# Transposing the gated FFN tiles of a hybrid trunk layer by DMA in 16-bit halves

## The chip, the cores and the metric

The kernel runs on one core of a Trainium2 chip. The metric is the device time of one execution in microseconds (us), median of the runs. All arithmetic of the layer is float32; nothing is computed on the host.

## The reference

One layer on `x` of 256 tokens by 2048 features, with `D_FF` = 5504: a half-step SwiGLU FFN, a mixer, a second half-step FFN, each between two RMS norms. The change touches the two FFNs alone.

```python
def rms_norm(x, w):
    y = xf * lax.rsqrt(jnp.mean(xf * xf, axis=-1, keepdims=True) + EPS)
    return (y * w.astype(jnp.float32)).astype(x.dtype)

def swiglu(x, w_gate, w_up, w_down):
    return (jax.nn.silu(x @ w_gate) * (x @ w_up)) @ w_down

def reference(...):
    f1 = swiglu(rms_norm(h, ffn1_pre_norm[l]), ffn1_w_gate[l], ffn1_w_up[l], ffn1_w_down[l])
    h = h + 0.5 * rms_norm(f1, ffn1_post_norm[l])
    m = hybrid_token_mixer(rms_norm(h, mix_pre_norm[l]), ...)
    h = h + rms_norm(m, mix_post_norm[l])
    f2 = swiglu(rms_norm(h, ffn2_pre_norm[l]), ffn2_w_gate[l], ffn2_w_up[l], ffn2_w_down[l])
    h = h + 0.5 * rms_norm(f2, ffn2_post_norm[l])
    return h
```

## The kernel before

The 256 tokens are two tiles `t` of 128 partitions. Every float32 matmul is three matmuls in the type float32r: a weight chunk `raw` is rounded on ScalarE to `whi` (line 151), VectorE takes the rest `wlo = raw - whi` (line 153), and `mm3` adds `xhi*whi`, `xlo*whi` and `xhi*wlo` (lines 157 to 159). The activations are kept transposed (`xhi`, `xlo`: features on partitions), since a matmul contracts over partitions.

An FFN goes over `D_FF` in ten blocks of 512 columns and one of 384 (`for f0`). In a block, `gemm_pair` makes the gate `g` and the up product `u` of both token tiles from 16 row blocks of each weight. Most row blocks are taken in plain steps (12 matmuls of a chunk of 1024 columns). Some are taken in steps of `seven`, in which seven products stand for eight: VectorE first makes sums of weights in `wsum` (line 243), ScalarE rounds `raw` and `wsum` (`whi` at lines 278 and 282, `wsumh` at 280 and 284), and VectorE takes the rests (`wlo` twice, `wsuml` once, all at line 243); TensorE then has 21 matmuls. Blocks alternate between three such steps (`SUMS`) and four (`FOUR`). At a block's end VectorE adds shared sums into the four results (`c<-c,psum`). The ring of `raw`, `whi` and `wlo` has five buffers each; `wsum`, `wsumh` and `wsuml` share a ring of three, so a step's `wsumh` waits until TensorE has read the last step's.

A block's end is then: ScalarE makes `silu` of the gate (line 728), and a generator `finish` per token tile does the rest. Its first step runs at once: VectorE multiplies `u`, the norm's factor and the silu into `hn` (line 703). Two of the generator's steps later TensorE transposes `hn` in pieces of 128x128 (line 397, four per tile, three in the last block) into a PSUM tile, and ScalarE copies that into `hT` (line 709), whose tiles stay in SBUF until the down projection splits them into `hkhi` and `hklo`. `side.pump()` after every plain step, and twice in a seven-product step, advances all generators by one step; `side.flush()` in the down projection's second step runs the last two to their end.

In each engine's queue the instructions stand in an order that a scheduler makes at build time from the order of the code and its own estimates, so a changed instruction also moves its neighbours; each engine then works off its queue in order. Weight loads are issued from SP's queue, a few others from ScalarE's. DMAs take eight completion semaphores in turn.

Of the kernel before, what the change touches and what calls it, by code (L numbers as in the profile page):

```python
# [7 lines left out]
F32 = mybir.dt.float32  # L8
F32R = mybir.dt.float32r
BF16 = mybir.dt.bfloat16  # L10
U8 = mybir.dt.uint8
AF = mybir.ActivationFunctionType
ALU = mybir.AluOpType
AX = mybir.AxisListType

P = 128
# [6 lines left out]
CB = 512  # L23
# [63 lines left out]
def kernel(ctx: ExitStack, tc: tile.TileContext, a: dict, out: bass.AP):  # L87
    nc = tc.nc
# [8 lines left out]
    work = ctx.enter_context(tc.tile_pool(name="work", bufs=2))  # L97
# [5 lines left out]
    def nm(s):  # L103
        uid[0] += 1
        return f"{s}_{uid[0]}"

    def ps_tile(s="ps"):
        return psum.tile([P, CB], F32, tag="ps", name=nm(s))

    h = [[hpool.tile([P, CB], F32, name=f"h{t}_{n}") for n in range(4)] for t in range(NT)]  # L110
# [13 lines left out]
    def ring_alloc(w):  # L124
        hi, lo = [ring.tile([P, RW], F32R, tag=s, name=nm(s))[:, :2 * w]
                  .rearrange("p (i c) -> p i c", i=2) for s in ("whi", "wlo")]
        return [(hi, lo)]
# [22 lines left out]
    def split_into(hi, lo, src):  # L150
        last[0] = nc.scalar.activation(hi, src, AF.Copy)  # L151
        with tc.issue_after(first_ops.pop().ins) if first_ops else nullcontext():
            nc.vector.tensor_tensor(lo, src, hi.bitcast(F32), op=ALU.subtract)  # L153
# [7 lines left out]
    def gemm_block(w_dram, c0, w, lhs, nkt=KT, held=None, raws=(), ready=()):  # L161

        raws, ready = list(raws), list(ready)
        nb = -(-w // CB)
        step = 2 // nb
        pss = [[ps_tile(f"mm{t}") for _ in range(nb)] for t in range(NT)]

        def chunk(k0, alloc):
            if ready:
                return ready.pop(0)
            raw = raws.pop(0) if raws else None
            src = w_dram[k0 * P:(k0 + step) * P, c0:c0 + w]
            return wchunk(src.rearrange("(k p) c -> p k c", p=P) if nb == 1 else
                          src.rearrange("p (n c) -> p n c", n=nb), w // nb, alloc, raw)

        def mm(t, k0, parts):
            for i, part in enumerate(parts):  # L180
                kt = k0 + i % step
                mm3(pss[t][i // step][:, :w // nb], lhs(t, kt), part, kt == 0, kt == nkt - 1)

        if held is None:
            for k0 in range(0, nkt, step):
                parts = chunk(k0, ring_alloc)
                for t in range(NT):
                    mm(t, k0, parts)
                side.pump()
        else:  # L190
            kept = []
            for i, k0 in enumerate(range(0, nkt, 2)):
                kept.append((k0, chunk(k0, ring_alloc if i < RING else held)))
                mm(0, *kept[-1])
                side.pump()
            for k in kept:
                mm(1, *k)
                side.pump()
            side.flush()
        return pss if nb > 1 else [ps[0] for ps in pss]  # L200
# [41 lines left out]
    def add(o, x, y, op=ALU.add):  # L242
        return nc.vector.tensor_tensor(o, x, y, op=op)  # L243

    class Blocks:
# [19 lines left out]
        def seven(self, u, end):  # L265
# [11 lines left out]
            (ahi, alo), (bhi, blo) = ring_alloc(w) + ring_alloc(w)  # L277
            nc.scalar.activation(ahi, ra, AF.Copy)  # L278
            add(wsum[:, 0:2, :], ra, rb[:, 0:1, :].broadcast_to([P, 2, w]))
            nc.scalar.activation(hi[:, 0:2, :], wsum[:, 0:2, :], AF.Copy)  # L280
            add(rb[:, 0, :], wsum[:, 0, :], ra[:, 1, :])
            nc.scalar.activation(bhi, rb, AF.Copy)  # L282
            summed = add(wsum[:, 2, :], rb[:, 0, :], rb[:, 1, :])
            last[0] = nc.scalar.activation(hi[:, 2, :], wsum[:, 2, :], AF.Copy)  # L284
            with tc.issue_after(summed.ins):
# [43 lines left out]
    def gemm_pair(ws, w, lhs, sums, ready=(), following=(), raws=(), sevens=SUMS,  # L329
                  late=False):  # L330

        raws = list(raws)
        nu = KT // 2

        b = Blocks(lambda i, kt: ws[i][0][kt * P:(kt + 1) * P, ws[i][1]:ws[i][1] + w],
                   w, lhs, part_of(sums))

        def split(i, k0):
            return wchunk(None, w, raw=raws.pop(0)) if raws else first_of(*ws[i], w)(k0 // 2)

        steps = [(u, i) for u in range(nu) if u not in sevens for i in range(2)]
        if late:
            at = range(6, 6 + 2 * len(sevens), 2)
        elif len(sevens) > len(SUMS):
            at = range(3, 3 + 2 * len(sevens), 2)  # L350
        else:
            at = [2 * u - j for j, u in enumerate(sevens)]
        for j, u in zip(at, sevens):
            steps.insert(j, (u, None))
        ready = list(ready)
        for j, (u, i) in enumerate(steps):
            side.fast = late
            if any(i is None for _, i in steps[j:j + 2]):
                side.full = True
            if i is None:  # L360
                b.seven(u, u == sevens[-1])
                continue
            k0 = 2 * u
            parts = ready.pop(0) if ready else split(i, k0)
            if (u, i) == (nu - 1, 0) and sevens:
                ready = [split(1, k0)]
                b.share()
            for t in range(NT):
                b.plain((k0, k0 + 1), t, i, parts, u == nu - 1)
            side.pump()  # L370
        ready = [chunk(0) for chunk in following]
        for i in range(2 if sevens else 0):
            for t in range(NT):
                b.close(t, i)
        side.full = side.fast = False
        return *[[b.c[t][i] for t in range(NT)] for i in range(2)], ready
# [18 lines left out]
    def transpose4(dst_ps, src, n=4):  # L395
        for i in range(n):
            end = nc.tensor.transpose(dst_ps[:, i * P:(i + 1) * P], src[:, i * P:(i + 1) * P],  # L397
                                      ident)
        return end

    def tiles4(x):
        return x.rearrange("p (k c) -> p k c", c=P)

    def new_xT():
        x = [None] * NT, [None] * NT, [0] * NT
        for t in range(NT):
            alloc_xT(x, t)
        return x
# [41 lines left out]
    def square(src, ss, n):  # L450
        sq = work.tile([P, CB], BF16, tag="sq", name=nm("sq"), bufs=1)
        nc.scalar.activation(sq, src, AF.Square, accum_out=ss[:, n:n + 1])

# [221 lines left out]
    def ffn(pre, x, rs, post, pre_next, begin=None, ready=(), then=None):  # L675
        with ExitStack() as fctx:
            fwork = fctx.enter_context(tc.tile_pool(name=nm("fwork"), bufs=2, reuse_waits="tile"))
# [19 lines left out]
            hT = []  # L697
# [1 line left out]
            fours = 0 if begin else 1  # L699

            def finish(t, f0, w, u, s):
                hn = fwork.tile([P, CB], F32, tag="hn", name=nm("hn"))
                nc.vector.scalar_tensor_tensor(hn[:, :w], u[:, :w], rs[t], s[:, :w],
                                               op0=ALU.mult, op1=ALU.mult)
                yield
                yield
                tp = ps_tile()
                transpose4(tp, hn, w // P)
                nc.scalar.activation(hT[f0 // CB][:, :w // P, t * P:(t + 1) * P],
                                     tiles4(tp[:, :w]), AF.Copy)  # L710

            for f0 in range(0, DFF, CB):
                w = min(CB, DFF - f0)
# [3 lines left out]
                if f0 or begin:  # L717
                    g, u, ready = gemm_pair(
                        [(a[pre + "_w_gate"], f0), (a[pre + "_w_up"], f0)], w, xl, sums, ready,
                        following, () if f0 else raws,  # L720
                        (FOUR if f0 // CB % 2 == fours else SUMS) if f0 else ())
# [3 lines left out]
                s = []  # L725
# [4 lines left out]
                if not (f0 or begin):  # L730
                    side.spawn(x_sums())
                    u = gemm_block(a[pre + "_w_up"], f0, w, xl)
# [40 lines left out]
                v = in_x("xhi1", F32R)  # L773
                return [(v[:, 0:2, :], v[:, 2:4, :])]

            ytags = ["hn", "hn", "silu", "silu"]

            def ys():
                return fwork.tile([P, CB], F32, tag=ytags.pop(), name=nm("y"))
# [6 lines left out]
    def mixer(x, rs, ready, following):  # L786
        xl = lhs_of(x)
        w_in = a["w_in"]
        with ExitStack() as mctx:
# [339 lines left out]
            for r0 in range(0, P, 32):  # L1129
                nc.vector.tensor_copy(diag[r0:r0 + 32, :], ident[r0:r0 + 32, r0:r0 + 32])  # L1130
            masks = mp.tile([P, masked, 4, 16], U8, name="masks")
            for i in range(4):
# [138 lines left out]
    x, rs = new_xT(), [None, None]  # L1271

    def begin(x_sums):
# [27 lines left out]
        def idling(n):  # L1301
            for _ in range(n):
# [7 lines left out]
        return raws  # L1310

    x, rs, ready = ffn("ffn1", x, rs, "ffn1_post_norm", wcols[:, 1, :], begin,
                       then=first_of(a["w_in"], O_GQ))
    x, rs, ready = mixer(x, rs, ready, first_of(a["ffn2_w_gate"], 0))
    ffn("ffn2", x, rs, "ffn2_post_norm", None, ready=ready)
    side.flush()

# [45 lines left out]
```

## Time and profile before

| | |
|---|---|
| runs | 2080.27 us median of 3 (2080.07 to 2080.61) |
| the profiled execution | 2080.67 us, its span 2078.8 us |
| granted TensorE clock over the span | 0.999 |
| first FFN, blocks | about 10 to 444 us |
| first FFN, down projection | about 444 to 685 us |
| mixer | about 685 to 1390 us |
| second FFN, blocks, then down projection | about 1390 to 1850 us, then to the end |

Times in a view are us from the span's start. In a row of the order of time stand the start, the duration, the engine, the line, the operation and `out<-in` by the program's names; `x2` is two equal instructions merged; in brackets stands the idle time just before it and what ended it. PE is TensorE's matmuls, PEld its weight loads, DVE VectorE, ACT ScalarE; an engine name with q is its queue, where DMAs are issued. Matmuls overlap: a 512-column matmul is shown with 0.39 us, while the next starts 0.23 us later.

### The profile page before, as it was taken

What the parts mean: (1) busy time and instruction counts of PE and PEld (TensorE: products, weight loads), DVE (VectorE), ACT (ScalarE), POOL (GpSimd) and SP (SyncE); (2) the same over time, 40 slices, a digit from 0 to 9 for tenths busy, and PEclk for the clock granted to TensorE, in tenths of its full rate; (3) what the DMA queues carried; (4) which work ended last, traced back from release to release, by engine and by line L of the source; (5) the groups of instructions that cost most, each with busy time, mean ns of one, the idle gap of its engine ahead of it and who ended that gap; (6) DMA issues with size and microseconds to landing.
All of it is one profiled execution on the core that took longest, in us unless ns stands there. A gap on an engine that the chain in (4) does not pass through costs nothing.

```text
span 2078.8 us, 29319 instructions
## 1 busy us (share of the span) xinstructions
PE 2067.8 (99%) x10509; PEld 1721.1 (83%) x10509; DVE 1854.7 (89%) x2187; ACT 1239.7 (60%) x1670; POOL 40.6 (2%) x87
## 2 busy tenths in 40 slices
PE   9999999999999999999999999999999999999998
PEld 7888888898888888878888888888888888898886
DVE  7898999989999879989999897578999989999896
ACT  6555656565666576576655554465555655666663
POOL 1000000000000100000000000010000000000000
PEclk9999999999999999999999999999999999999999
DMA  8566656656667467555565666755666657576663
GB/s 267 183 210 199 211 188 194 214 183 226 208 195 233 153 192 232 163 168 188 174 203 186 184 221 214 220 179 172 222 200 186 209 186 224 165 239 201 198 208 132
DMA packets 200665, 412.23 MB, mean 198 GB/s; under 512 B 18036, under 2 KB 26423, under 8 KB 200520
## 3 DMA queue, kind: packets, MB, share of 16 engines
q1 hardware_dynamic: 194896, 401.80, 61.0%
q10 hardware_dynamic: 5624, 8.57, 1.3%
q8 instruction: 82, 1.34, 0.3%
q14 instruction: 63, 0.52, 0.1%
HBM read 406.11 MB, written 4.19 MB: 197 GB/s over the span
## 4 chain that ended last, share of the span: by engine, by line
PE 96%; ACT 1%; DVE 1%; issue 0%; DMA 0%; POOL 0%; SPq 0%; DVEq 0%; POOLq 0%; ACTq 0%
PE c L157 22%; PE c L159 21%; PE c L158 21%; PE p L159 5%; PE p L158 5%; PE p L157 5%; PE mm L157 3%; PE mm L159 3%; PE mm L158 3%; PE ps L397 2%; PE acc L157 1%; PE acc L158 1%; PE acc L159 1%; PE ps L905 0%; DVE h L510 0%
## 5 line engine op out<-in xcount | busy, mean ns | idle before, releaser
L151 ACT ACTIVATE whi<-raw 128x1024 fp32r<-128x1024 f32 (+3 forms) x498 | 510.6, 1033 | 279.8 <-PE c L158 114.7
L153 DVE TENSOR_TENSOR wlo<-raw,whi 128x1024 fp32r<-128x1024 f32 (+3 forms) x498 | 587.5, 1190 | 86.6 <-ACT whi L151 85.3
L157 PE MATMUL c<-whi,xhi 128*128 128x512 f32 (+1 forms) x1270 | 495.8, 391 | 0.5 <-DVE hq L849 0.3
L159 PE MATMUL c<-wlo,xhi 128*128 128x512 f32 (+1 forms) x1270 | 490.8, 387 | 0.0
L158 PE MATMUL c<-whi,xlo 128*128 128x512 f32 (+1 forms) x1270 | 490.5, 386 | 0.0
L243 DVE TENSOR_TENSOR wlo<-raw,whi 128x1024 fp32r<-128x1024 f32 (+1 forms) x252 | 294.5, 1203 | 11.9 <-ACT whi L278 6.3
L159 PEld LDWEIGHTS c<-wlo,xhi 128*128 128x128 f32 x1270 | 238.4, 188 | 47.2 <-DVE wlo L153 0.3
L157 PEld LDWEIGHTS c<-whi,xhi 128*128 128x128 f32 x1270 | 238.5, 188 | 46.9 <-issue 0.7
L158 PEld LDWEIGHTS c<-whi,xlo 128*128 128x128 f32 x1270 | 238.6, 188 | 44.9
L282 ACT ACTIVATE whi<-raw 128x1024 fp32r<-128x1024 f32 (+1 forms) x126 | 131.8, 1046 | 204.5 <-DVE raw L243 78.5
L243 DVE TENSOR_TENSOR wsuml<-wsum,wsumh 128x1536 fp32r<-128x1536 f32 (+1 forms) x126 | 218.0, 1730 | 33.7 <-ACT wsumh L284 33.6
L157 PE MATMUL c<-whi,hkhi 128*128 128x512 f32 x558 | 217.0, 389 | 0.0
L159 PE MATMUL c<-wlo,hkhi 128*128 128x512 f32 x558 | 216.8, 388 | 0.0
L158 PE MATMUL c<-whi,hklo 128*128 128x512 f32 x558 | 216.7, 388 | 0.0
L280 ACT ACTIVATE wsumh<-wsum 128x1024 fp32r<-128x1024 f32 (+1 forms) x126 | 131.5, 1044 | 108.6 <-DVE wsum L243 74.7
L278 ACT ACTIVATE whi<-raw 128x1024 fp32r<-128x1024 f32 (+1 forms) x126 | 131.4, 1043 | 100.2 <-PE c L158 84.7
L243 DVE TENSOR_TENSOR wsum<-raw,raw 128x1024 f32<-128x1024 f32 (+1 forms) x126 | 151.8, 1205 | 20.5 <-DMA raw<-in_ffn_w_down_dram 17.3
L159 PEld LDWEIGHTS c<-wlo,hkhi 128*128 128x128 f32 x558 | 104.8, 188 | 21.6
L158 PEld LDWEIGHTS c<-whi,hklo 128*128 128x128 f32 x558 | 104.8, 188 | 21.3
L157 PEld LDWEIGHTS c<-whi,hkhi 128*128 128x128 f32 x558 | 104.8, 188 | 21.3
L243 DVE TENSOR_TENSOR c<-c,psum 128x512 f32<-128x512 f32 (+1 forms) x135 | 86.6, 682 | 11.8 <-PE c L159 11.4
L243 DVE TENSOR_TENSOR wsum<-raw 128x512 f32<-128x512 f32 (+1 forms) x126 | 86.0, 683 | 3.6
(347 smaller groups left out, 3117.1 us busy)
## 6 DMA issues: line engine op xcount, KB each, us to landing
raw<-in_ffn_w_down_dram SPq DMA_DIRECT2D x124, 512.0 KB, 4.6
raw<-in_w_in_dram SPq DMA_DIRECT2D x104, 512.0 KB, 4.5
raw<-in_ffn_w_up_dram SPq DMA_DIRECT2D x97, 512.0 KB, 4.5
raw<-in_ffn_w_gate_dram SPq DMA_DIRECT2D x96, 512.0 KB, 4.7
raw<-in_ffn_w_gate_dram SPq DMA_DIRECT2D x128, 256.0 KB, 3.8
raw<-in_w_in_dram SPq DMA_DIRECT2D x128, 256.0 KB, 3.5
raw<-in_ffn_w_up_dram SPq DMA_DIRECT2D x126, 256.0 KB, 3.8
raw<-in_ffn_w_down_dram SPq DMA_DIRECT2D x96, 256.0 KB, 4.0
```

The source lines that it names most:

```text
L151: last[0] = nc.scalar.activation(hi, src, AF.Copy)
L153: nc.vector.tensor_tensor(lo, src, hi.bitcast(F32), op=ALU.subtract)
L157: nc.tensor.matmul(ps, lhsT=xhi, rhs=whi, start=start, stop=False)
L158: nc.tensor.matmul(ps, lhsT=xlo, rhs=whi, start=False, stop=False)
L159: nc.tensor.matmul(ps, lhsT=xhi, rhs=wlo, start=False, stop=stop)
L243: return nc.vector.tensor_tensor(o, x, y, op=op)
L278: nc.scalar.activation(ahi, ra, AF.Copy)
L280: nc.scalar.activation(hi[:, 0:2, :], wsum[:, 0:2, :], AF.Copy)
L282: nc.scalar.activation(bhi, rb, AF.Copy)
L397: end = nc.tensor.transpose(dst_ps[:, i * P:(i + 1) * P], src[:, i * P:(i + 1) * P], ident)
```

## The change

`finish` no longer uses TensorE. VectorE writes the gated tile over the silu tile. ScalarE reads that tile as 16-bit words, two for each float32, and writes the low halves of all columns and then the high halves into `halves` (two planes of 512 values, as whole numbers in uint16). A DMA transpose, issued from ScalarE's queue, turns the eight blocks of 128x128 (six in the last block) into `turned`. Six generator steps later ScalarE writes the planes back into every second 16-bit word of `hT`. `turned` uses the three buffers of the tag `tmp`, and the down projection's `y` tiles use the tag `halves` where they used `hn`.

```diff
             def finish(t, f0, w, u, s):
-                hn = fwork.tile([P, CB], F32, tag="hn", name=nm("hn"))
-                nc.vector.scalar_tensor_tensor(hn[:, :w], u[:, :w], rs[t], s[:, :w],
+                n = w // P
+                nc.vector.scalar_tensor_tensor(s[:, :w], u[:, :w], rs[t], s[:, :w],
                                                op0=ALU.mult, op1=ALU.mult)
                 yield
-                yield
-                tp = ps_tile()
-                transpose4(tp, hn, w // P)
-                nc.scalar.activation(hT[f0 // CB][:, :w // P, t * P:(t + 1) * P],
-                                     tiles4(tp[:, :w]), AF.Copy)
+                halves = fwork.tile([P, 2 * CB], U16, tag="halves", name=nm("halves"))
+                nc.scalar.activation(halves[:, :2 * w].rearrange("p (h f) -> p h f", h=2),
+                                     s.bitcast(U16)[:, :2 * w].rearrange("p (f h) -> p h f", h=2),
+                                     AF.Copy)
+                turned = work.tile([P, 8, P], U16, tag="tmp", name=nm("turned"), bufs=3)
+                nc.scalar.dma_start_transpose(turned[:, :2 * n, :], halves[:, :2 * w])
+                for _ in range(6):
+                    yield
+                dst = hT[f0 // CB].bitcast(U16)[:, :n, 2 * t * P:2 * (t + 1) * P]
+                src = turned[:, :2 * n, :].rearrange("p (h j) k -> p h j k", h=2)
+                nc.scalar.activation(dst.rearrange("p j (k h) -> p h j k", h=2), src, AF.Copy)
...
-            ytags = ["hn", "hn", "silu", "silu"]
+            ytags = ["halves", "halves", "silu", "silu"]
```

The scheduler puts the new instructions so. ScalarE's queue at the start of the first FFN's third block, which has four seven-product steps (98 to 137 us), before:

```order
L280 ACTIVATE wsumh_1021<-wsum_1020 128x1024
L282 ACTIVATE whi_1029<-raw_1019 128x1024
L284 ACTIVATE wsumh_1021<-wsum_1020 128x512
L151 ACTIVATE whi_1068<-raw_1066 128x1024
L278 ACTIVATE whi_1093<-raw_1084 128x1024
L709 ACTIVATE hT_955<-ps_988 128x4x128
L709 ACTIVATE hT_955<-ps_994 128x4x128
L282 ACTIVATE whi_1095<-raw_1085 128x1024
L151 ACTIVATE whi_1130<-raw_1128 128x1024
L278 ACTIVATE whi_1155<-raw_1146 128x1024
L280 ACTIVATE wsumh_1087<-wsum_1086 128x1024
```

And with the change, at the same place. Lines from 12 on are one higher in the changed file, those behind `finish` seven; the text names lines of the kernel before.

```order
L281 ACTIVATE wsumh_1011<-wsum_1010 128x1024
L708 ACTIVATE halves_970<-silu_947 128x1024
L708 ACTIVATE halves_974<-silu_949 128x1024
L712 DMA_TRANSPOSE turned_972<-halves_970 128x8x128
L712 DMA_TRANSPOSE turned_976<-halves_974 128x8x128
L283 ACTIVATE whi_1019<-raw_1009 128x1024
L285 ACTIVATE wsumh_1011<-wsum_1010 128x512
L152 ACTIVATE whi_1058<-raw_1056 128x1024
L279 ACTIVATE whi_1083<-raw_1074 128x1024
L717 ACTIVATE hT_951<-turned_972 128x2x4x128
L717 ACTIVATE hT_951<-turned_976 128x2x4x128
L283 ACTIVATE whi_1085<-raw_1075 128x1024
```

Both `halves` and both transposes stand ahead of the step's second weight rounding; `hT` keeps its place, four activations behind the transposes. In blocks with three such steps the same four stand ahead of the first `wsumh` instead. Behind these rows ScalarE's order differs too: from the block's second seven-product step on, both `wsumh` stand ahead of the plain step's `whi`. VectorE follows; its queue in that second step, before:

```order
L243 TENSOR_TENSOR wlo_1094<-raw_1084,whi_1093 128x1024
L243 TENSOR_TENSOR wlo_1096<-raw_1085,whi_1095 128x1024
L153 TENSOR_TENSOR wlo_1131<-raw_1128,whi_1130 128x1024
L243 TENSOR_TENSOR wsuml_1088<-wsum_1086,wsumh_1087 128x1536
L243 TENSOR_TENSOR wsum_1148<-raw_1146,raw_1147 128x1024
```

With the change:

```order
L244 TENSOR_TENSOR wlo_1084<-raw_1074,whi_1083 128x1024
L244 TENSOR_TENSOR wlo_1086<-raw_1075,whi_1085 128x1024
L244 TENSOR_TENSOR wsuml_1078<-wsum_1076,wsumh_1077 128x1536
L154 TENSOR_TENSOR wlo_1123<-raw_1120,whi_1122 128x1024
L244 TENSOR_TENSOR wsum_1140<-raw_1138,raw_1139 128x1024
```

`wsuml` and the plain step's `wlo` have changed places; this is so in all steps of the four-step blocks but the first. In the first FFN's last block (384 columns) the results of the block before it are turned closer together on ScalarE, with the change:

```order
L708 ACTIVATE halves_3778<-silu_3755 128x1024
L152 ACTIVATE whi_3866<-raw_3864 128x768
L712 DMA_TRANSPOSE turned_3780<-halves_3778 128x8x128
L708 ACTIVATE halves_3782<-silu_3757 128x1024
L279 ACTIVATE whi_3891<-raw_3882 128x768
L712 DMA_TRANSPOSE turned_3784<-halves_3782 128x8x128
L717 ACTIVATE hT_3759<-turned_3780 128x2x4x128
L283 ACTIVATE whi_3893<-raw_3883 128x768
L717 ACTIVATE hT_3759<-turned_3784 128x2x4x128
```

Here and in the two down projections only one or two activations stand between a transpose and the `hT` that waits for it. TensorE's queue differs by the missing transposes alone, SP's and GpSimd's not at all.

More of the change, by code (lines that the diff above doesn't have):

```diff
@@ L11 @@
 U8 = mybir.dt.uint8
+U16 = mybir.dt.uint16
 AF = mybir.ActivationFunctionType
```

## Prediction

> **What bounds the kernel now.** I read the page's engine lines and its chain first, then two stretches of the first FFN side by side, then the order of time of each engine in them.
>
> ```profile
> PE 2067.8 (99%) x10509; PEld 1721.1 (83%) x10509; DVE 1854.7 (89%) x2187; ACT 1239.7 (60%) x1670; POOL 40.6 (2%) x87
> ...
> PE 96%; ACT 1%; DVE 1%; issue 0%; DMA 0%; POOL 0%; SPq 0%; DVEq 0%; POOLq 0%; ACTq 0%
> ```
>
> ```profile
> 98.00:137.00 39.00, 39.00 (x178) 32.37 (x177) 37.32 (x37) 22.35 (x26) 0.00 (x0) 1.00 0.60 191
> 137.00:177.00 40.00, 40.00 (x183) 33.19 (x182) 36.35 (x37) 23.07 (x27) 0.00 (x0) 1.00 0.66 210
> ```
>
> The two window rows are a block with four seven-product steps (98 to 137) and one with three (137 to 177); after the span's stretch come PE, PEld, DVE, ACT and POOL busy, then clock, DMA share and GB/s. TensorE has no gap in either, at full clock, so time taken off TensorE is time won as long as its operands are there. VectorE, at 37.32 of 39, is the engine that could fail to keep up. ScalarE has 17 us free in each, but VectorE's residues wait for its roundings, so what counts is where its new work stands.
>
> **What is removed.** First the tile views of `hn` and `hT` (durations as min, median, max), then one row of the chain in order of time (start, share of the chain):
>
> ```profile
> L397 PE MATMUL ps<-ident,hn x172: 270/272/273, 59.8 to 1849.7; 128*128 128x128 f32 x172
> L709 ACT ACTIVATE hT<-ps x44: 465/580/592, 60.8 to 1850.5; 128x512 f32<-128x512 f32 x40, 128x384 f32<-128x384 f32 x4
> ```
>
> ```profile
> 1815.34 0.87 PE ps L397 x8
> ```
>
> 172 transposes go. Their 272 ns overlap; the chain gives what a set of eight costs TensorE, 0.87 us. So the most that can be won is 172 / 8 x 0.87 = **18.7 us** (the 272 ns of the tile view summed without overlap would be 47, which no stretch without gaps could give back). VectorE's gating product keeps its size and only writes over the silu tile.
>
> **What is added on ScalarE.** Per gated tile: two activations of 1024 elements and one DMA issue, for one activation of 0.58. The trace has none with 16-bit data at a step of two; a 128x1024 activation takes 1.04 to 1.06 (L278 and L282 below), the 580 ns row is the low end, twice 1.06 the high one. I take 1.04, the same number of elements. That is 44 x (2 x 1.04 - 0.58) = 66 us, 3 us per block of two tiles beside 17 us free. So not the sum but the place decides. ScalarE and VectorE in order of time there (start, duration, idle before it):
>
> ```profile
> 96.84 1.06 ACT L280 ACTIVATE wsumh<-wsum 128x1024 fp32r<-128x1024 f32 x1 [0.19 <-DVE wsum L243]
> 100.07 1.06 ACT L282 ACTIVATE whi<-raw 128x1024 fp32r<-128x1024 f32 x1 [2.17 <-PE c L159]
> 101.04 0.61 ACT L284 ACTIVATE wsumh<-wsum 128x512 fp32r<-128x512 f32 x1
> 101.56 1.04 ACT L151 ACTIVATE whi<-raw 128x1024 fp32r<-128x1024 f32 x1
> 102.65 1.06 ACT L278 ACTIVATE whi<-raw 128x1024 fp32r<-128x1024 f32 x1
> ```
>
> ```profile
> 97.99 1.40 DVE L703 SCALAR_TENSOR_TENSOR hn<-c,r,silu 128x512 f32<-128x512 f32 x2
> ...
> 100.64 2.35 DVE L243 TENSOR_TENSOR wlo<-raw,whi 128x1024 fp32r<-128x1024 f32 x2
> ```
>
> In the four-step block the order puts both `halves` and both transposes between L280 and L282. The gating products end at about 98.7 and 99.4. `halves` runs 98.7 to 99.7 and 99.7 to 100.7; the first issue can start at 99.7, the second at 100.7 or when the first lets go. With X for the time one issue holds ScalarE's queue, the rounding L282 starts at 99.7 + 2X instead of 100.07. Queued behind it are L284, L151 and L278; waiting for it is the second `wlo` of the pair, which VectorE reaches at 101.8. VectorE's delay is D = 99.7 + 2X + 1.06 - 101.8 = **2X - 1.0**. What issues and landings cost here, from the list of DMAs, the view of line 385 and SP's order of time:
>
> ```profile
> held<-in_ffn_post_norm_dram ACTq DMA_DIRECT2D x8, 256.0 KB, 4.9
> away<-h SPq DMA_DIRECT2D x8, 256.0 KB, 2.0
> ```
>
> ```profile
> L385 ACTq DMA_DIRECT2D held<-in_ffn_post_norm_dram x8: 334/334/357, 478.9 to 1862.1; - x8
> ...
> DMA to landing us min/median/max: 4.2/4.9/7.3
> ```
>
> ```profile
> 132.87 1.04 SPq L274 DMA_DIRECT2D raw<-in_ffn_w_up_dram  x1
> ```
>
> No DMA transpose is in this trace. X is bounded below by a plain issue on this queue, 0.33, and above by an issue that holds the queue until its data is there: 2.0 from SBUF, 4.9 (7.3 at worst) from HBM. I take 1.04, the longest issue shown, since eight 128x128 blocks have to be turned, not one copied. Then D = 1.1. Does TensorE feel it? That is read from how far `wsuml` is ahead of the product that reads it:
>
> ```profile
> 102.91 1.75 DVE L243 TENSOR_TENSOR wsuml<-wsum,wsumh 128x1536 fp32r<-128x1536 f32 x1
> ...
> 112.66 1.76 DVE L243 TENSOR_TENSOR wsuml<-wsum,wsumh 128x1536 fp32r<-128x1536 f32 x1 [0.88 <-ACT wsumh L284]
> ...
> 121.02 1.76 DVE L243 TENSOR_TENSOR wsuml<-wsum,wsumh 128x1536 fp32r<-128x1536 f32 x1 [0.50 <-ACT wsumh L284]
> 122.82 1.23 DVE L243 TENSOR_TENSOR wsum<-raw,raw 128x1024 f32<-128x1024 f32 x1
> ...
> 128.82 1.75 DVE L243 TENSOR_TENSOR wsuml<-wsum,wsumh 128x1536 fp32r<-128x1536 f32 x1
> 130.49 2.35 DVE L153 TENSOR_TENSOR wlo<-raw,whi 128x1024 fp32r<-128x1024 f32 x2
> ```
>
> ```profile
> 109.43 0.39 PE L159 MATMUL p<-wsuml,hkhi 128*128 128x512 f32 x1
> ...
> 116.91 0.39 PE L159 MATMUL p<-wsuml,hkhi 128*128 128x512 f32 x1
> ...
> 131.87 0.39 PE L159 MATMUL p<-wsuml,hkhi 128*128 128x512 f32 x1
> ```
>
> The first is ready at 104.66 and read at 109.43, 4.77 ahead; the fourth at 130.57 and read at 131.87, **1.30 ahead**. A step takes TensorE 116.91 - 109.43 = 7.48 and VectorE 121.02 - 112.66 = 8.36, with waits for L284 in it; that drains the lead. Without waits the same seven instructions take 130.49 - 122.82 = 7.67. The moved order (`wsuml` ahead of the plain `wlo`, L280 and L284 ahead of L151 and L278) takes those waits out from the second step on. So the lead at the fourth becomes 4.77 - 0.87 (TensorE comes earlier) - D - 3 x 0.19 = 3.3 - D = 2.2: no stall, and none until X passes 2.2 us.
>
> In the three-step block the issues stand ahead of L280:
>
> ```profile
> 139.75 1.40 DVE L703 SCALAR_TENSOR_TENSOR hn<-c,r,silu 128x512 f32<-128x512 f32 x2
> ```
>
> ```profile
> 143.51 1.06 ACT L280 ACTIVATE wsumh<-wsum 128x1024 fp32r<-128x1024 f32 x1 [3.19 <-DVE wsum L243]
> ```
>
> `halves` ends at 142.4, the second issue at about 143.6: the idle 3.19 us hides it.
>
> **Where the result comes back.** `hT` now waits for the landing. In the four-step block L282, L284, L151 and L278 stand in between, 3.6 us, so the first `hT` comes at 105.4 and the second at 106.4, 5.7 us after their issues: both landing rows of 256 KB, 2.0 and 4.9, fit. [...] The shortest distances are at three places, the first FFN's last block and the two starts of the down projection. There only an activation or two stand between, about 2.9 us with the issue: between 0 (landing 2.0) and 2.0 us of standing (landing 4.9), behind which the next weight's rounding queues. I charge **4 us** in all. The transposes add 0.5 MB to a block's 39 us at 191 GB/s, 7.4 MB: hidden by a DMA share of 0.60; without that cover `raw` would land later and ScalarE wait.
>
> **Sum**, against the profiled execution's own 2080.67 us (0.4 above the median of 2080.27): 2080.7 - 18.7 + 4 = **2066**.
>
> **The rivals.**
>
> - *The issue holds ScalarE (slower).* Place: L282 in the ten four-step blocks. Against it: every DMA issue in the trace ends within 1.04. For it: none there turns eight blocks. It costs 10 x (2X - 4.3): it decides from X = 2.2 and eats the gain of 15 at X = 2.9; at X = 4.2, the fastest HBM landing, 41 us, **2107**.
> - *The transfers go one behind the other and land late (slower).* With two landings of 7.3 the second `hT` of the four-step block starts at 99.7 + 14.6 = 114.3; then L282, L280 and L284 (2.6) and `wsuml` (1.75) end at 119.7, where TensorE wants it at 116.9 - 0.9: 3.7 us in each of ten blocks, and about 10 at the three close places: 2080.7 - 18.7 + 37 + 30 = **2129**. [...]
> - *Only half is won.* If L280, which now stands ahead of L151 and waits for TensorE to have read the last `wsumh`, keeps VectorE at 8.36 a step, the lead is 4.77 - 0.87 - D - 3 x 0.88 = 1.3 - D: about 0.7 us is lost in ten blocks at X = 1.5, **2073**.
>
> **How the numbers follow.** About 0.2%, 4 us, can be told from no change. Forecast, 2060 to 2072: 0.57. Half is won: 0.12, nearly all still faster. An issue near X = 2.9, within 4 us of before: 0.11. Slower by the first two rivals: 0.20. That gives faster 0.68, same 0.12, slower 0.20. The low end is all 18.7 us with nothing charged, and a little; the high end takes in X up to about 3.6 and leaves 0.13 above it and 0.03 below: 2060 to 2095.
>
> **What would show it.** Right: no TensorE gap over 0.2 us in blocks of either kind, DMA_TRANSPOSE issues near 1 us, landing under 5.7 us, no wait of ScalarE at the second `hT` except at the three places, `halves` near 1.04. Wrong: issues over 2.2 us with gaps before `wsuml`'s product every 80 us (first rival); ScalarE idle before `hT` in all 22 blocks (second); gaps in four-step blocks with short issues (third). Activations much above 1.04 us on 16-bit data would also make it wrong.

## The result and the profile after

The changed kernel takes 2071.34 us (median of 4 runs, 2070.85 to 2072.41), the kernel before 2080.44 us beside it (4 runs, 2080.07 to 2081.21). The ratio is 0.9957, with a 95% interval of 0.9942 to 0.9972: 9.1 us faster, where the forecast was 2066 and so some 14 us. The profiled execution of the changed kernel took 2072.41 us, with a span of 2070.3. Of the 18.7 us that the transposes cost TensorE, about half came out.

The page's engine line of the changed kernel, and the tile view of `turned` (durations as min, median, max):

```profile
PE 2054.9 (99%) x10337; PEld 1701.7 (82%) x10337; DVE 1849.8 (89%) x2187; ACT 1303.3 (63%) x1714; POOL 40.7 (2%) x87
```

```profile
L712 ACTq DMA_TRANSPOSE turned<-halves x44: 1227/1292/2006, 56.3 to 1838.5; - x44
L717 ACT ACTIVATE hT<-turned x44: 1062/1361/1394, 61.7 to 1847.5; 128x1024 uint16<-128x1024 uint16 x40, 128x768 uint16<-128x768 uint16 x4
...
  DMA turned<-halves: 24.3, 16
...
DMA to landing us min/median/max: 2.8/5.1/8.9
```

One issue holds ScalarE's queue for 1.29 us, a landing takes 5.1 us (median) and up to 8.9 as far as the trace tells it (22 of the 44), and in 16 of 44 cases ScalarE stands idle in front of `hT`, 24.3 us in all. The same two stretches as in the prediction, cut 0.9, 1.8 and 2.7 us earlier, where the same matmuls stand now (columns as there):

```profile
97.10:135.20 38.10, 38.10 (x169) 31.55 (x169) 35.98 (x36) 25.59 (x28) 0.00 (x0) 1.00 0.68 199
135.20:174.30 39.10, 39.10 (x174) 32.36 (x173) 37.26 (x38) 25.86 (x29) 0.00 (x0) 1.00 0.78 238
```

TensorE is busy all through both, so each set of eight transposes gives its 0.9 us there. The gain comes in the blocks. Where it is lost again shows when the same matmul (counted without the transposes) is looked up in the order of time of TensorE in both kernels. Before:

```profile
447.13 0.33 PE L158 MATMUL c<-whi,hklo 128*128 128x384 f32 x1
...
530.10 0.39 PE L159 MATMUL c<-wlo,hkhi 128*128 128x512 f32 x1
...
1800.11 0.39 PE L157 MATMUL c<-whi,xhi 128*128 128x512 f32 x1
...
1905.10 0.39 PE L158 MATMUL p<-wsumh,held 128*128 128x512 f32 x1
```

And after:

```profile
438.05 0.33 PE L159 MATMUL c<-whi,hklo 128*128 128x384 f32 x1
...
526.25 0.39 PE L160 MATMUL c<-wlo,hkhi 128*128 128x512 f32 x1
...
1789.09 0.39 PE L158 MATMUL c<-whi,xhi 128*128 128x512 f32 x1
...
1896.54 0.40 PE L159 MATMUL p<-wsumh,held 128*128 128x512 f32 x1
```

In the first FFN's last block (which runs to about 469 us in the kernel before, where its last gating product ends, and not to the 444 of the table of stages) TensorE is 9.08 us ahead of the kernel before, ten sets at 0.91. Behind the start of its down projection it is only 3.85 ahead. Near the end of the second FFN's blocks it is 11.02 ahead, in its down projection 8.56. So 5.2 and 2.5 us are given back on balance, each within some 100 us around the end of an FFN's blocks. What is lost is more, since a set of six transposes (0.7 us) is still won in the first stretch, and a set of eight and one of six (1.6 us) in the second: 5.9 and 4.1 us. These are the places to which the prediction charged 4 us, with the second FFN's last block and the rest of the down projections besides.

The first down projection's start, ScalarE in order of time in the changed kernel, and the one long wait of TensorE in it:

```profile
461.68 0.56 ACT L735 ACTIVATE silu<-c,r 128x384 f32<-128x384 f32 x1
462.14 1.63 ACT L708 ACTIVATE halves<-silu 128x768 uint16<-128x768 uint16 x2
463.00 2.58 ACTq L712 DMA_TRANSPOSE turned<-halves  x2
465.68 1.06 ACT L152 ACTIVATE whi<-raw 128x1024 fp32r<-128x1024 f32 x1 [1.91 <-issue]
466.64 1.06 ACT L717 ACTIVATE hT<-turned 128x768 uint16<-128x768 uint16 x1
469.88 1.08 ACT L717 ACTIVATE hT<-turned 128x768 uint16<-128x768 uint16 x1 [2.17 <-DMA turned<-halves]
470.82 1.04 ACT L279 ACTIVATE whi<-raw 128x1024 fp32r<-128x1024 f32 x1
```

```profile
464.08 0.50 PE L160 MATMUL c<-wlo,hkhi 128*128 128x512 f32 x1 [2.01 <-DVE wlo L154]
```

The product `c<-wlo,hkhi` that waits here is the one that some expectations below call the product at 468 us; by this profile's clock it is at 464.08. Three causes offer themselves: the issues hold ScalarE for 2.6 us, `hT` waits 2.2 us for its landing with a weight's rounding behind it, and TensorE, coming 9 us earlier, may be early for weights that can't be there yet. The experiments tell them apart.

### The profile page after: what moved, and what is told of

It is laid out like the page before. It is cut to its first block, busy times and chain, and to the rows that moved or that the text cites. A ratio compares the mean times of both kernels' runs of the same rounds, so it can differ in the third digit from the quotient of the medians.

```text
span 2070.3 us, 28990 instructions
## 1 busy us (share of the span) xinstructions
PE 2054.9 (99%) x10337; PEld 1701.7 (82%) x10337; DVE 1849.8 (89%) x2187; ACT 1303.3 (63%) x1714; POOL 40.7 (2%) x87
## 3 DMA queue, kind: packets, MB, share of 16 engines
q8 instruction: 81, 1.33, 0.3%
```

## The experiments

All ran three rounds beside the kernel before, whose medians lay between 2080.24 and 2080.46.

| run | edit | us, median (lowest to highest) | ratio to before [95%] |
|---|---|---|---|
| e1 | kernel before, no transposes at all | 2064.94 (2063.69 to 2065.91) | 0.9924 [0.9907, 0.9940] |
| e2 | last two blocks back on TensorE | 2064.59 (2064.53 to 2064.70) | 0.9924 [0.9909, 0.9939] |
| e3 | `hT` later in the down projection | 2067.45 (2067.40 to 2069.10) | 0.9940 [0.9925, 0.9955] |
| e4 | transposes issued on SP's queue | 2064.29 (2063.84 to 2068.79) | 0.9927 [0.9913, 0.9942] |
| e5 | no transfers, activations kept | 2065.32 (2063.65 to 2066.10) | 0.9926 [0.9912, 0.9941] |
| e6 | transfers made, landing not awaited | 2065.13 (2064.79 to 2065.40) | 0.9926 [0.9912, 0.9941] |
| e7 | e3 and e4 together | 2065.38 (2063.61 to 2067.24) | 0.9928 [0.9913, 0.9943] |
| e8 | e4, last block on TensorE | 2066.63 (2066.34 to 2067.01) | 0.9934 [0.9918, 0.9951] |
| e9 | e4, first FFN's blocks changed over | 2060.04 (2060.00 to 2060.24) | 0.9902 [0.9887, 0.9917] |
| e10 | kernel before, blocks changed over | 2080.57 (2080.11 to 2081.37) | 1.0001 [0.9992, 1.0011] |
| e11 | `hT` ten steps later, and e3 | 2067.10 (2065.85 to 2068.64) | 0.9936 [0.9921, 0.9951] |
| e12 | blocks changed over alone | 2070.46 (2067.49 to 2072.67) | 0.9946 [0.9930, 0.9963] |

### e1: what there is to win

```diff
                 yield
                 yield
-                tp = ps_tile()
-                transpose4(tp, hn, w // P)
                 nc.scalar.activation(hT[f0 // CB][:, :w // P, t * P:(t + 1) * P],
-                                     tiles4(tp[:, :w]), AF.Copy)
+                                     tiles4(hn[:, :w]), AF.Copy)
```

> Kernel before with TensorE's 172 transposes of hn left out: ScalarE copies hn straight into hT, so the FFN output is computed from tiles that aren't transposed. It bounds what taking that work off TensorE can win. Theory A (the changed kernel loses its missing gain because ScalarE's added work and waits stand in the way at the blocks' end and the down projection's start): nothing of that is added here, so the whole 18.7 us come out, 2061 to 2063 us. Theory B (the down projection's start can't use a TensorE that comes 9 us earlier, since weights and VectorE's residues aren't there yet): some 5 us per FFN are handed back here too, 2070 to 2073 us.

2064.94 lies between the two. With no transfer at all, 15.4 us come out, not 18.7. TensorE waits at one product, in the first FFN's down projection, the very product of the changed kernel's gap:

```profile
463.35 0.80 PE L159 MATMUL c<-wlo,hkhi 128*128 128x512 f32 x1 [3.13 <-DVE wlo L153]
463.95 0.63 PE L158 MATMUL c<-whi,hklo 128*128 128x512 f32 x1
```

So some 3 us of the missing gain have nothing to do with the transfers; the other 6.4 (2071.34 - 2064.94) do. e5 and e6 show which part of them. In e1's profile the loss at this product is larger than 3 us: TensorE's lead over the kernel before falls from 9.06 to 4.76 us, while a set of six is won, so 5.0 are lost, 1.6 of them to a lower clock (last section). The 3 us come out smaller since there was more to win than 18.7 us, as the account of the prediction shows.

### e5 and e6: a ladder from no transfer to a landing that is awaited

In e6 only the source of `hT` is another in the code; in e5 the transfers go too.

```diff
-                src = turned[:, :2 * n, :].rearrange("p (h j) k -> p h j k", h=2)
+                src = halves[:, :2 * w].rearrange("p (h j k) -> p h j k", h=2, k=P)
```

```diff
-                turned = work.tile([P, 8, P], U16, tag="tmp", name=nm("turned"), bufs=3)
-                nc.scalar.dma_start_transpose(turned[:, :2 * n, :], halves[:, :2 * w])
```

> Changed kernel without the 44 transfers: ScalarE makes halves and, six steps later, writes hT from halves, so the two longer activations stay and neither an issue nor a landing is left; hT isn't transposed. First rung of a ladder up to the changed kernel. Theory A (issues and landings are the loss): as the kernel without transposes, 2064 to 2066 us. Rival (the activations' own 3 us per block): 2068 to 2071 us.

> Changed kernel with all its instructions, the 44 transposes among them, but hT is written from halves and waits for no landing; hT isn't transposed. Second rung: what lies between this and the run without transfers is the issues' hold of ScalarE and the traffic, what lies between this and the changed kernel is the wait for the landing. Theory A1 (the landing, 24 us of ScalarE's idle time in all): 2065 to 2067 us. Theory A2 (the hold, 1.3 us per issue): 2069 to 2071 us.

The rungs are e1 2064.94, e5 2065.32, e6 2065.13, changed kernel 2071.34. The longer activations cost nothing that can be told, nor do the 44 issues and their traffic, with 1.3 us of ScalarE's queue each. The wait for the landing costs **6.2 us**, all of the rest, with the order that the scheduler makes for it: in e6 it puts some `hT` ahead of a rounding, and 63 of ScalarE's 1714 activations stand at another place than in the changed kernel. That the transfers of e6 were no quicker shows its tile view of `turned`:

```profile
DMA to landing us min/median/max: 2.8/5.1/8.8
```

In the two profiles, 7.6 us apart, e6 is 2.5 us ahead of the changed kernel where the second FFN starts, so most of the loss lies in the second FFN. ScalarE's longest wait in front of `hT` is at its down projection's start. TensorE's lead over the kernel before falls from 11.3 to 9.4 us behind it, in many short waits, of which the longest is shown second, both in the changed kernel:

```profile
1845.58 1.07 ACT L717 ACTIVATE hT<-turned 128x768 uint16<-128x768 uint16 x1 [4.09 <-DMA turned<-halves]
```

```profile
1850.74 0.50 PE L160 MATMUL p<-wlo,hkhi 128*128 128x512 f32 x1 [0.53 <-DVE wlo L244]
```

### e3 and e11: giving the landing more room

In e3 the down projection only makes one step where it flushed, and flushes at its tenth step; in e11 `range(6)` is `range(10)` as well.

```diff
                 if not hf and kt == 1:
-                    side.flush()
+                    side.pump()
+                if not hf and kt == 9:
+                    side.flush()
```

> Changed kernel; in the down projection the halves and the transposes stay in its second step, but hT is written from turned in its tenth step instead of right behind them. Theory A1 (what costs there is ScalarE's wait for the landing, 2.2 us in the first FFN): that wait goes, and with it 2 us per FFN, 2066 to 2068 us. Theory A2 (what costs is that halves and the two issues, 4.2 us, stand ahead of the weight roundings): the gap of TensorE of 2.0 us at 468 us stays, 2070 to 2072 us.

> Changed kernel, issues on ScalarE's queue as in it, but hT is written ten generator steps behind the transposes instead of six, and in the down projection in its tenth step. Theory A1 (only the wait for the landing costs): with the landing's 5.1 us (median) covered everywhere it is as fast as the kernel that awaits no landing, 2064 to 2066 us. Theory A2 (the issue's hold of ScalarE costs too): no faster than with the later write in the down projection alone, 2067 to 2068 us.

e3 wins 3.9 us, as A1 said, about two thirds of what the landing costs: there are waits in the last blocks too. But the gap at the product of 464 us is still there with 1.56 us, which only A2 had asked for; e5 shows it as well, with no issue at all, so the gap is not A2's but that of e1. e11 misses: it is no better than e3. Its view of `turned` says why it can't decide:

```profile
  DMA turned<-halves: 16.6, 6
...
DMA to landing us min/median/max: 3.2/5.4/11.9
```

Its landings reached 11.9 us, so there were still 16.6 us of waiting, at 6 places now. The room grew, and the landing with it.

### e4 and e7: the other queue

```diff
-                nc.scalar.dma_start_transpose(turned[:, :2 * n, :], halves[:, :2 * w])
+                nc.sync.dma_start_transpose(turned[:, :2 * n, :], halves[:, :2 * w])
```

> Changed kernel with the 44 transposes issued from SP's queue, where the weight loads are issued, instead of ScalarE's. Theory A2 (ScalarE is held by the issues, 1.3 us each, where the roundings are close): ScalarE gets 2.6 us per set back, 1 to 2 us per FFN at the close places, 2067 to 2070 us. Rival: SP's queue, held for each issue and waiting for halves, lets the weight loads behind it go later; VectorE and ScalarE then wait for raw, 2074 us or more.

2064.29, better than either theory said. The tile view of `turned` in e4:

```profile
L712 SPq DMA_TRANSPOSE turned<-halves x44: 1217/1240/2222, 56.5 to 1832.1; - x44
...
  DMA turned<-halves: 8.6, 9
...
DMA to landing us min/median/max: 2.7/3.1/4.9
```

An issue holds SP's queue as long as it held ScalarE's, but the landing falls from 5.1 to 3.1 us in the median and from 8.9 to 4.9 at worst, and the waiting from 24.3 to 8.6 us. By the ladder, where the issues cost nothing, it isn't ScalarE's freed queue that gives the 7 us but the shorter landing; e4 alone changes both, and the order of 144 activations with them. Why the landing is shorter is taken up in the last section. e7 joins e3's edit to it:

> Changed kernel with the transposes issued from SP's queue and, in the down projection, hT written in the tenth step. If the two losses add up: 2061 to 2063 us, better than either alone. If TensorE, coming 9 us earlier, must wait at the first FFN's down projection for weights that land late in any case (3.3 us at one product in the kernel without transposes): 2063.5 to 2065 us, no better than the issue on SP alone.

2065.38, the second case and 0.4 over: no better than e4, and the gap at that product (1.99 us in e7) stays.

### e2 and e8: the ends of the FFN back on TensorE

```diff
+                if f0 >= 9 * CB:
+                    yield
+                    tp = ps_tile()
+                    transpose4(tp, s, n)
+                    nc.scalar.activation(hT[f0 // CB][:, :n, t * P:(t + 1) * P],
+                                         tiles4(tp[:, :w]), AF.Copy)
+                    return
                 halves = fwork.tile([P, 2 * CB], U16, tag="halves", name=nm("halves"))
```

In e8 the bound is `10 * CB`, with the transposes on SP's queue.

> Changed kernel, but the results of each FFN's last two blocks are transposed on TensorE as before; the first nine blocks of each FFN keep the DMA. Theory A (the loss sits in ScalarE's work at the last block and the down projection's start): 18 of 22 sets are won at 0.9 us, nothing is lost, 2063 to 2066 us, better than both kernels. Theory B (the down projection's start hands back whatever was won before it): no better than the changed kernel, 2070 to 2073 us.

> Changed kernel with the transposes issued from SP's queue, but each FFN's last block (384 columns, two of the 22 sets of an execution) transposed on TensorE. 20 of 22 sets at 0.91 us are 18.2 us, 2062 us, if nothing is lost at the first FFN's down projection any more; 2064 to 2066 us if the weights land late there however the last block is transposed.

e2 is right by theory A: 18 sets are won on ScalarE's queue, and nothing is lost at the FFNs' ends. Its 36 landings still took up to 8.8 us, and ScalarE still waited 11.8 us for them. In the blocks that costs TensorE little: 18 sets at 0.91 us are 16.4, and the run came out 15.7 us below the kernel before beside it. e8, with two more sets on the DMA, is no better: 2.3 us above e4's median and 0.6 above the range of its second case. 1.4 us of the 2.3 are what the two sets of six cost that stay on TensorE (2 x 0.68). Its TensorE waits 2.39 us at the same product again.

### e9, e10 and e12: why that product waits

```diff
-            fours = 0 if begin else 1
+            fours = 1
```

> Changed kernel with the transposes issued from SP's queue, and in the first FFN three- and four-step blocks changed over, so that its last, narrow block has three steps (as in the second FFN, whose down projection loses nothing with this issue). Theory C (the product at 468 us waits since the narrow four-step block ahead of it uses up VectorE's lead, so that buffers for the down projection's weights come free late): the 3 us lost there come back, 2060 to 2062.5 us. Rival (the weights land late there whatever the block ahead): 2064 to 2066 us.

> Control to the run before this: kernel before with only the first FFN's three- and four-step blocks changed over. Theory C: the kernel before loses nothing at that product, so only the seven-product steps of a 384-column block become those of a 512-column one; within 2 us of before, 2078 to 2081 us. If it gains as much as the changed kernel does by it, the gain belongs to the order of the blocks and not to the loss at that product.

> Changed kernel, issues on ScalarE's queue as in it, with only the first FFN's three- and four-step blocks changed over. Fourth corner of a square of two edits (queue of the issue, order of the blocks). If the wait for the landing and the lost lead at the first FFN's down projection are separate losses, they add up: 2071.3 - 4.3 = 2067 us. If they are one loss counted twice, this edit alone brings most of the 11 us that both together bring: 2061 to 2064 us. If the landing alone sets the time: 2070 to 2072 us.

With the blocks changed over and the issue on SP's queue the kernel takes **2060.04 us**, the fastest of all: 4.3 us below e4 and 20.3 below the kernel before beside it. The same edit alone leaves the kernel before where it was (1.0001, 0.9992 to 1.0011), so it gains only where TensorE comes earlier. So the loss at that product goes with the blocks' order, once TensorE comes early enough: e2 keeps the order and, 8.2 us ahead instead of 9.1, loses nothing there. The 20.3 us are also more than the prediction's most, 18.7: at the 0.91 us that a set of eight is worth in the blocks, 172 transposes are 19.6 us. The remaining 0.7 us stays unexplained. How the loss comes about is read from e1, where ScalarE and VectorE stand shortly before the product:

```profile
458.52 1.06 ACT L151 ACTIVATE whi<-raw 128x1024 fp32r<-128x1024 f32 x1 [3.44 <-DMA raw<-in_ffn_w_down_dram]
```

```profile
460.08 0.62 DVE L703 SCALAR_TENSOR_TENSOR hn<-c,r,silu 128x384 f32<-128x384 f32 x1 [2.70 <-ACT silu L726]
```

A weight of the down projection lands late; `silu` is queued behind its rounding, and the residues behind the gating product that waits for `silu`. Its load in turn had waited for a buffer. It was slow besides: issued at 451.7 us, it landed 6.7 us later; of the 512 KB loads from 441 to 472 us the median landing was 6.2 us in e1 and 4.8 in e2. Waits of SP's queue for VectorE's residues from 441 to 472 us (total, times, longest), in e1 and in e9:

```profile
SPq L133 <- DVE wlo L243: 16.2, 5, 5.7
...
SPq L272 <- DVE wlo L153: 8.8, 1, 8.8
```

```profile
SPq L134 <- DVE wlo L244: 9.7, 4, 5.6
...
SPq L273 <- DVE wlo L154: 1.2, 1, 1.2
```

That fits theory C, buffers coming free late behind a narrow four-step block; that VectorE's lead is the cause of the late landing is argued from these rows and not tried by itself, and the 6.7 us of the load are not explained by it. That `silu` stands behind a rounding in ScalarE's queue is part of the wait as well; another order there was not tried. The stretch from 440 to 530 us in the changed kernel and in e9:

```profile
440.00:530.00 90.00, 86.86 (x395) 72.16 (x396) 81.76 (x107) 56.93 (x73) 0.00 (x0) 1.00 0.67 207
```

```profile
440.00:530.00 90.00, 90.00 (x421) 77.35 (x420) 81.84 (x108) 58.22 (x73) 0.00 (x0) 1.00 0.70 225
```

TensorE stands 3.1 us in the first and not at all in the second. e12's median of 2070.46 lies in its third case, but its four runs lie 5.2 us apart, two at 2067.5 and 2068.3 (near the first case) and two at 2072.6 and 2072.7, so it doesn't decide between these two cases; the second is out. In its profile, one of the long runs, the gap at that product is gone, and the wait for the landing stops TensorE further on instead, in both down projections: 3.9 and 6.1 us of its lead go there. ScalarE and TensorE in the second:

```profile
1842.95 1.07 ACT L717 ACTIVATE hT<-turned 128x768 uint16<-128x768 uint16 x1 [3.40 <-DMA turned<-halves]
1848.42 1.06 ACT L717 ACTIVATE hT<-turned 128x768 uint16<-128x768 uint16 x1 [4.40 <-DMA turned<-halves]
1849.35 1.03 ACT L279 ACTIVATE whi<-raw 128x1024 fp32r<-128x1024 f32 x1
```

```profile
1850.43 0.50 PE L158 MATMUL p<-whi,hkhi 128*128 128x512 f32 x1 [3.64 <-ACT whi L279]
```

This is the mechanism in one piece: `hT` itself isn't needed for long, but in ScalarE's queue it stands ahead of a rounding that TensorE needs at once. In such a run the two losses don't simply add up. While landings are awaited, the time that the block order gives is spent at the next of them; with short landings (e9) it is kept.

## Why the prediction was half right

- **What is removed** held: each set of eight transposes is worth 0.91 us in the blocks (9.08 for ten), against 0.87 in the chain. So the most that could be won was nearer 19.6 us than 18.7.
- **ScalarE's added work beside the blocks** held. `halves` took 1.04 us as taken; `hT` took 1.36 where I had taken 1.04, and that is hidden too, as e5 shows.
- **X** was 1.29 to 1.33 us, where I took 1.04 as the longest issue shown. (The trace of before has longer ones: 1.48 us at L275 on SP's queue; on ScalarE's 0.49 is the longest.) ScalarE and VectorE in the four-step block after:

```profile
98.92 2.65 ACTq L712 DMA_TRANSPOSE turned<-halves  x2
101.70 1.06 ACT L283 ACTIVATE whi<-raw 128x1024 fp32r<-128x1024 f32 x1 [1.85 <-PE c L159]
...
105.08 2.57 ACT L717 ACTIVATE hT<-turned 128x1024 uint16<-128x1024 uint16 x2
```

```profile
111.60 1.75 DVE L244 TENSOR_TENSOR wsuml<-wsum,wsumh 128x1536 fp32r<-128x1536 f32 x1
...
119.26 1.75 DVE L244 TENSOR_TENSOR wsuml<-wsum,wsumh 128x1536 fp32r<-128x1536 f32 x1
...
126.92 1.75 DVE L244 TENSOR_TENSOR wsuml<-wsum,wsumh 128x1536 fp32r<-128x1536 f32 x1
```

```profile
130.02 0.39 PE L160 MATMUL p<-wsuml,hkhi 128*128 128x512 f32 x1
```

  The step's lead is 130.02 - 128.67 = 1.35 us at the fourth `wsuml`; with X at 1.32 the working gives 3.3 - 1.6 = 1.7. VectorE's steps are 7.66 us apart, so the moved order did take its waits out, and the third rival (half is won) falls, though its 2073 us came nearer to the measured time than the forecast did. The first rival needed X above 2.2 and falls as well.
- **The landing in the blocks** held for TensorE, though not as told: `hT` came at 105.08 with no idle time here, but ScalarE waited at 16 places, not at six. Most of the others lie where there is lead to spare. In one four-step block, the second FFN's second, there was too little. `hT` comes late there, roundings and `wsumh` behind it, and TensorE's lead falls from 4.6 to 4.0 us by 1464 us; e4 and e6 lose nothing at that place:

```profile
1439.86 1.37 ACT L717 ACTIVATE hT<-turned 128x1024 uint16<-128x1024 uint16 x1 [2.63 <-DMA turned<-halves]
```

- **The step that failed** is the last term of the sum, "I charge 4 us in all" for the three close places. It was sized with landings of 2.0 to 4.9 us, which are those of plain transfers; that a transpose lands in the same time was the author's estimate and stood in no trace. On ScalarE's queue it took 5.1 us (median), up to 8.9, and of the gain 9.6 us are missing (18.7 less the 9.1 that came out); in the profiles 5.9 and 4.1 us are lost around the two ends. Of the 9.6 the wait for the landing is 6.2 us, where the one landing that the trace tells at the second down projection's start took 8.3 us. Some 3 us more, which the forecast didn't have at all, are lost in e1 without any transfer: I asked what is late next in the four-step block, but not at the down projection's first products, where TensorE arrives with the sum of ten blocks' gains, 9 us, and not 0.87. That 2071 still lies within the stated range is luck in part: its upper end was made for long issues, and those didn't come.
- **The second rival** was right in part: landings as long as its 7.3 us came, and of its 30 us at the three close places about a third. But the ten four-step blocks lost nothing like its 37 us (0.7 in the one named above, 1.8 in the first FFN's last), and eight 128x128 blocks landed in 3.1 us (median) on SP's queue and 5.1 on ScalarE's, issue included, against its 7.3. The 256 KB weight loads of the changed kernel land in 3.5 to 4.0 us (medians in its list of DMAs): the transposes of 256 KB land like them on SP's queue and later on ScalarE's.

## What to carry to other kernels

Time won block after block arrived at the next stage as one sum, 9.08 us here; ask of that stage's first products what is late when TensorE comes by the whole sum earlier. An operation that waits for a DMA should not stand, on a queue that works in order, ahead of something that is needed at once, whenever its own result is needed: in e12 4.40 us of waiting for a landing in front of a rounding stopped TensorE for 3.64. And the landing should be bounded by the longest row of the trace (here 8.9 us), not by a median (5.1). A move that gains little may still be worth its full price with its issue on another queue and the order around it changed: here 9 us became 20.

## What the runs showed of the hardware

The same transfer landed in 5.1 us (up to 8.9) from ScalarE's queue and in 3.1 us (up to 4.9) from SP's, where the weight loads are issued too. In the changed kernel the landing goes with the weight loads that SP's queue issues during it: with one such load it took 3.2 to 3.3 us (four cases, at 181, 264, 1680 and 1762 us), with three 5.0 to 8.3 (seven cases), with five or six 6.5 to 8.9 (five cases); with two or four it lies between 2.8 and 8.0. In e4, where the loads issued meanwhile stand behind the transpose on the same queue, the landing lay between 2.7 and 4.9 us, as far as the trace tells it. That speaks for loads on the other queue as what lengthens the landing here; no run tries that by itself, and by what means stays open.

A pause of TensorE cost more than its length in some runs. After the 3.13 us in e1 the granted clock (last but two) was

```profile
463.30:466.80 3.50, 3.45 (x8) 2.78 (x9) 3.50 (x6) 0.37 (x1) 0.00 (x0) 0.51 0.60 179
```

and in these 3.5 us eight matmuls ran where 0.23 us apart would have taken 1.8, so 1.6 us more were lost. The pause's length alone doesn't decide. Behind pauses of 3.82 us (e5), 3.13 (e1) and 1.87 (e6) the clock stood at 0.50 for about 3.4 us, as windows of 1 us give it; behind one of 3.64 in e12, with 0.52 just after it, matmuls started 0.43 us apart from 1852.3 to 1854.4 us, as they did in e1 at that clock, and 0.23 apart afterwards. Behind 2.01 us in the changed kernel and 2.39 in e8 it stayed at 1.00. The runs of one kernel differ in this too: e4's longest, 2068.79 us, had a mean clock of 0.997, its others 0.999. So the rungs of the ladder hold such losses as well as waits: e1, e5 and e6 had one in their profiles, the changed kernel none.
